# The chunk scan with compact states, 64x64 tiles and TensorE in the written order

## The chip, the core and the metric

The kernel runs on one core of one Trainium2 chip. The metric is the time of one execution on the device in microseconds (us). PE is TensorE, PEld its weight loads, DVE is VectorE, ACT ScalarE, POOL GpSimd, SP the engine that issues most transfers. Everything is float32. A product of two float32 operands stands in the trace as two matmul instructions, one after the other; a transpose is one.

## What is computed

The reference is a two-layer trunk over 512 latent and 256 context tokens of width 1024. The change touches one part of layer 0, the time mixing: eight heads of 64 features, each with a recurrence over the tokens, once forwards and once backwards.

```python
def rwkv7_scan(f, d, s0, reverse):
    def step(state, inp):
        r_t, w_t, k_t, v_t, kk_t, a_t = inp
        sa = jnp.einsum('bhvk,bhk->bhv', state, -kk_t)
        state = (state * w_t[:, :, None, :] + sa[..., None] * (kk_t * a_t)[:, :, None, :]
                 + v_t[..., None] * k_t[:, :, None, :])
        return state, jnp.einsum('bhvk,bhk->bhv', state, r_t)
    ...
    s_last, ys = lax.scan(step, s0, xs, reverse=reverse)
```

Before it stand the projections of the input and the factors r, w, k, v, kk, a; after it a group norm, a bonus, a gate, the output projection and the feed-forward block; then layer 1. The modulation of both layers (a product of the conditioning vector with 24 blocks of 512 columns) is computed beside.

## The kernel before

**Pairs and chunks.** The heads are worked on in four pairs (p = 0 to 3), two heads on the 128 partitions. The 768 tokens are cut into 12 chunks of 64, and the recurrence over a chunk is written as products of 64-row matrices. `chunks` (L983) walks the 12 chunks of a pair in both directions at once, in three steps per chunk:

1. `cha` gets the right-hand sides `pr` for both heads h and both directions d: four products of the chunk matrix Gs with Z (L1050) and two of AR with the state S (L1053); ACT copies them to `rr`. Then `pre_g` makes the chunk matrix Gs two chunks ahead: two products of 128 rows by 256 columns (L1003) against `bd`, a block-diagonal copy of AR that `pre_d` has ACT write (four copies for every two chunks), and a masked copy on DVE (L1005).
2. `chb` gets four 64x64 products of the inverse XI with `rr` (L1064); ACT copies them into Z in two halves, one per direction. Two products of AR with S start the output `py` (L1069). Every second chunk follow `pre_t` (four transposes, L1012) and `pre_v` (L1024).
3. `chb` gets two 128x128 products of bt with Z (L1076); four DVE instructions (L1086) make the next state S of them and of `sw`, which POOL scales before (L1081). Four products (L1092) finish the output, which ACT or DVE adds to y (L1100).

The state S is [128, 2, 128]: for each direction a 128x128 block in which only the two 64x64 blocks of the two heads are not zero. The chain from one chunk to the next is S, L1053, rr, L1064, Z, L1076, S.

**Tilings of the array.** The form in the trace names the rows and columns of the array that a product uses: 128*128 in L1003, L1012 and L1076, 128*64 in L1050, L1053, L1069, L1024 and L1092, 64*64 in L1064 and L903, 32*32 in L963 and L971, 128*2 in the modulation (L344), 2*128 in its transposition (L354).

**Beside the scan.** The loop over the pairs advances three generators: `cg`, the scan of pair p; `bg`, in 1.8 steps per step of `cg`, which holds `prep` of pair p+1 (chunk factors; L903 with a masked copy on DVE, L904, six times; an inverse by 62 small DVE instructions, L925 and L926, ended by a copy, L929; three trips of the blocks through DRAM; the merges L963 and L971), `mix_out` of pair p-1 and the first part of `prep` of pair p+2; and `ag`, the modulation (L344, 16 matmul instructions per step). The scan of pair p+1 needs the merged XI.

**What sets the order.** Outside blocks of a written order a scheduler puts each engine's instructions in order at build time, from priorities (the order in which the code runs), what is ready by its own estimate, and free buffers. At run time each engine works through its list and waits where an operand is missing. PSUM has eight banks here: two single tiles `one`, one pair of banks `wide` (L903 and others of `prep` use it), two single `cha`, one `chb` and one `pad` for the modulation.

## Time and profile before

| | us |
|---|---|
| median of 3 runs (2109.83 to 2113.08) | 2113.08 |
| span of the profiled execution | 2117.1 |
| scan of pair 0 to the start of pair 1 (383 to 482) | 99 |
| pair 1 (482 to 587.6) | 105.6 |
| pair 2 (587.6 to 677) | 89.4 |
| pair 3 (677 to 755) | 78 |
| the four pairs together | 372 |

The profiled execution's span is 4.0 us above the median, 0.2%; the two are not the same run. The edges of the four stretches are the first DVE instructions that write a state (L1088). A busy share of PE is read with care: a matmul that waits behind another for the array counts as busy, and its end is modelled.

### The profile page before, as it was taken

Reading aid. Unit: us, or ns where it says so; the run is one execution under the profiler, and the core shown is the slowest. Engines: PE = TensorE matmul, PEld = TensorE weight load, DVE = VectorE, ACT = ScalarE, POOL = GpSimd, SP = SyncE. Lnnn points to the kernel's source line nnn. Section 1 sums busy time; section 2 is a strip of 40 time slices with the busy share of each in tenths; the row PEclk is TensorE's granted clock in tenths of the full one; section 3 lists DMA queues with packets and bytes.
Section 4 is the critical chain, followed back from the end, with each engine's and each line's share of the span. In section 5 each row is a group of like instructions: output and inputs, shape, how many; then the busy total and the mean of one; then the engine's idle time right before and its main releaser. Section 6 shows DMA issues by size and latency. Waiting matters only on the chain.

```text
span 2117.1 us, 37174 instructions
## 1 busy us (share of the span) xinstructions
PE 2002.1 (95%) x15404; PEld 1674.9 (79%) x15404; DVE 1172.4 (55%) x2190; ACT 879.8 (42%) x1799; POOL 150.5 (7%) x202
## 2 busy tenths in 40 slices
PE   6899997989898999999999999989999899999997
PEld 4778875666665689888888889988878799888887
DVE  4575578565765438434334433674566656544445
ACT  3365533455454525332212222344677645322232
POOL 1000001112121100000000000001121000000000
PEclk7999998889898989999999999999999999999998
DMA  7432224544535624322212221134111424332231
GB/s 278 144 95 77 90 81 127 148 113 136 163 102 151 240 75 130 110 80 64 60 37 80 80 61 50 51 110 146 42 36 51 130 81 150 109 99 80 80 100 41
DMA packets 111434, 215.77 MB, mean 102 GB/s; under 512 B 38432, under 2 KB 63904, under 8 KB 110752
## 3 DMA queue, kind: packets, MB, share of 16 engines
q1 hardware_dynamic: 95968, 190.06, 28.9%
q10 hardware_dynamic: 15296, 23.33, 3.1%
q8 instruction: 121, 1.98, 0.4%
q14 instruction: 49, 0.40, 0.1%
HBM read 182.69 MB, written 28.05 MB: 100 GB/s over the span
## 4 chain that ended last, share of the span: by engine, by line
PE 80%; DVE 9%; ACT 4%; issue 3%; DMA 2%; POOL 1%; SPq 0%; ACTq 0%; POOLq 0%; DVEq 0%
PE x L1507 44%; PE x L422 9%; PE ax L522 3%; PE x L1003 2%; PE ax L503 2%; PE ad L344 2%; PE b L485 2%; PE chb L1076 1%; PE b L486 1%; PE cha L1092 1%; PE cha L1053 1%; PE chb L1064 1%; PE ad L354 1%; POOL r L258 1%; PE x L1012 1%
## 5 line engine op out<-in xcount | busy, mean ns | idle before, releaser
L179 ACT ACTIVATE w_hi<-w_raw 128x1024 fp32r<-128x1024 f32 x183 | 192.1, 1058 | 475.4 <-PE x L1507 362.7
L219 DVE TENSOR_TENSOR w_lo<-w_raw,w_hi 128x1024 fp32r<-128x1024 f32 x181 | 222.1, 1231 | 192.8 <-ACT w_hi L179 186.1
L1507 PE MATMUL x<-fl,w_hi 128*128 128x256 f32 (+1 forms) x864 | 291.7, 339 | 4.0 <-DVE fl L1594 3.9
L1507 PE MATMUL x<-uh,w_hi 128*128 128x512 f32 (+1 forms) x864 | 288.1, 339 | 3.0 <-ACT uh L179 3.0
L1507 PE MATMUL x<-fh,w_lo 128*128 128x256 f32 (+1 forms) x864 | 289.9, 337 | 0.0
L1507 PE MATMUL x<-ul,w_hi 128*128 128x512 f32 (+1 forms) x864 | 287.4, 336 | 0.0
L1507 PE MATMUL x<-uh,w_lo 128*128 128x512 f32 (+1 forms) x864 | 287.4, 335 | 0.0
L1507 PE MATMUL x<-fh,w_hi 128*128 128x256 f32 (+1 forms) x864 | 287.3, 338 | 0.0
L1521 DVE TENSOR_TENSOR oa<-x,oa 128x512 f32<-128x512 f32 (+1 forms) x184 | 103.0, 562 | 208.4 <-PE x L1507 207.8
L422 PE MATMUL x<-uh,w_hi 128*128 128x256 f32 (+1 forms) x560 | 188.4, 336 | 2.7 <-ACT po L179 2.3
L422 PE MATMUL x<-uh,w_lo 128*128 128x256 f32 (+1 forms) x560 | 187.6, 335 | 0.0
L422 PE MATMUL x<-ul,w_hi 128*128 128x256 f32 (+1 forms) x560 | 187.5, 335 | 0.0
L1507 PEld LDWEIGHTS x<-fl,w_hi 128*128 128x128 f32 x864 | 165.0, 191 | 22.4 <-DVE fl L1594 4.4
L1507 PEld LDWEIGHTS x<-fh,w_lo 128*128 128x128 f32 x864 | 164.7, 191 | 18.1
L1507 PEld LDWEIGHTS x<-uh,w_hi 128*128 128x128 f32 x864 | 161.9, 190 | 21.1 <-ACT uh L179 4.0
L1507 PEld LDWEIGHTS x<-fh,w_hi 128*128 128x128 f32 x864 | 162.5, 190 | 20.2 <-ACT fh L179 2.5
L1507 PEld LDWEIGHTS x<-uh,w_lo 128*128 128x128 f32 x864 | 163.0, 190 | 18.3
L1507 PEld LDWEIGHTS x<-ul,w_hi 128*128 128x128 f32 x864 | 162.7, 189 | 17.9
L422 PEld LDWEIGHTS x<-uh,w_hi 128*128 128x128 f32 x560 | 106.2, 190 | 11.8 <-ACT po L179 2.5
L422 PEld LDWEIGHTS x<-uh,w_lo 128*128 128x128 f32 x560 | 106.4, 190 | 9.2 <-issue 1.3
L422 PEld LDWEIGHTS x<-ul,w_hi 128*128 128x128 f32 x560 | 106.0, 189 | 8.8 <-issue 1.2
L1593 DVE TENSOR_TENSOR rl<-rl 128x512 f32<-128x512 f32 (+1 forms) x108 | 59.3, 550 | 75.5 <-ACT fh L179 75.3
(286 smaller groups left out, 3657.4 us busy)
## 6 DMA issues: line engine op xcount, KB each, us to landing
w_raw<-in_wf_dram SPq DMA_DIRECT2D x128, 512.0 KB
w_raw<-in_wada_dram SPq DMA_DIRECT2D x96, 512.0 KB
w_raw<-in_we_dram SPq DMA_DIRECT2D x21, 512.0 KB
w_raw<-in_wo_in_dram SPq DMA_DIRECT2D x18, 512.0 KB
w_raw<-in_wout_dram SPq DMA_DIRECT2D x16, 512.0 KB
hsc<-h ACTq DMA_DIRECT2D x8, 1024.0 KB
scr<-po ACTq DMA_DIRECT2D x21, 384.0 KB
h<-hsc SPq DMA_DIRECT2D x7, 1024.0 KB
```

The costliest lines, as they stand in the source:

```text
L179: return S.activation(o, i, f, **k)
L219: eng.tensor_tensor(o_lo, x, o_hi.bitcast(F32), op=ALU.subtract)
L258: G.tensor_tensor(dst, src, C["mhalf"][:, :n], op=ALU.pow)
L344: PE.matmul(ps[32 * j:32 * j + 2, 0:128], si[:, 2 * kp + k, :], w[:, k, j * 128:(j + 1) * 128], start=kp + k == 0, stop=kp == 3 and k == 1)
L422: PE.matmul(ps[:, 0:b - a], x, y, start=j == 0, stop=j == len(pairs) - 1)
L485: PE.matmul(ps[:, off:off + n], qs, kh, start=True, stop=False)
L503: PE.transpose(pt[:, (kb - k0) * 128:(kb - k0 + 1) * 128], P[:, kb * 128:(kb + 1) * 128], ident)
L522: PE.matmul(po[h * 64:h * 64 + 64, 0:128], v(h, k), pts[h][:, k], start=k == 0, stop=k == n - 1)
L1003: PE.matmul(pg[:, d].rearrange("p h t -> p (h t)"), BK[d][:, c, :], BD[:, i % 2, d].rearrange("p h t -> p (h t)"), start=True, stop=True)
L1507: PE.matmul(o, a, b, start=n == 0, stop=n == len(pairs) - 1)
L1521: tt(oa[:, m, tok], ps, oa[:, m, tok], op=ALU.add)
L1593: tt(r, r, r, op=ALU.mult)
```

## The change

Part by part (line numbers of after differ from those of before; the names don't):

- The state S becomes [128, 2, 64]: the heads on the two halves of the partitions, the block-diagonal zeros gone. `bd` and `pre_d` with its ACT copies go.
- `pre_g` makes Gs in eight products of 64 rows by 64 columns with 128 moving columns, over the four quadrants of the array, into the two banks of `wide` instead of one bank of `one`.
- The products of AR with S become four 64x64 products over the four quadrants for `pr` and four for `py`, both at the start of the chunk; `cha` takes two banks, one per head, and there is one `cha` instead of two.
- The products of Gs with Z for `pr` go ahead by a chunk (`pre_r`): ACT copies them to `r0`, and DVE adds the state's part (instead of an ACT copy of the sum).
- The two halves of Z are copied by ACT and by DVE (before: both by ACT).
- The products for the new state become four of 128 rows by 64 columns; two DVE instructions instead of four make S, and POOL's `sw` is issued in step 1 instead of step 3.
- `pre_v` stands in step 3, `pre_t` in step 2.
- In the loop over the pairs PE keeps the order in which the code is written; the other engines are ordered by the scheduler as before.

```diff
 def mix_state(sc):
-    SS = [sc.tile([128, 2, 128], F32, name=f"S{i}") for i in range(2)]
+    SS = [sc.tile([128, 2, 64], F32, name=f"S{i}") for i in range(2)]
...
-    def pre_d(ii):
-        for d, (c, e) in enumerate(pair(ii)):
-            for h in range(2):
-                hs = slice(h * 64, h * 64 + 64)
-                a = AR[d][hs, c:c + 2, :] if d == 0 else AR[d][hs, e:e + 2, :][:, ::-1, :]
-                act(BD[hs, :, d, h, :], a)
...
     def pre_g(i):
-        pg = one().rearrange("p (d h t) -> p d h t", d=2, h=2)
+        pg = wide().rearrange("p (h x) -> p h x", h=2)
         for d, c in enumerate((FWD[i], BWD[i])):
-            PE.matmul(pg[:, d].rearrange("p h t -> p (h t)"), BK[d][:, c, :], BD[:, i % 2, d].rearrange("p h t -> p (h t)"), start=True, stop=True)
+            for j in range(2):
+                for h in range(2):
+                    PE.matmul(pg[half(j), h, d * 128:d * 128 + 128], BK[d][half(h), c, half(j)], AR[d][half(h), c, :], start=True, stop=True)
...
+    def pre_r(i):
+        pz = one()[:, 0:128]
+        for h, d in HD:
+            PE.matmul(pz[half(d), half(h)], nxt["G", i][:, d, h, 0:64], ZZ[i // 2 % 2][:, i % 2, d, h, :], start=True, stop=True)
+        r0 = ct.tile([128, 128], F32, name="r0", bufs=2)
+        act(r0, pz)
...
-        cha = pch.tile([128, 512], F32, name="cha", bufs=2)
+        cha = pch.tile([128, 2, 512], F32, name="cha")
...
+        if i:
+            for h, d in HD:
+                PE.matmul(cha[half(d), h, 0:64], AR[d][half(h), cd[d], 0:64], St[half(h), d, :], start=True, stop=True)
+            r0, rr = rr, ct.tile([128, 128], F32, name="rr")
+            tt(rr.rearrange("p (h v) -> p h v", h=2), cha[:, :, 0:64], r0.rearrange("p (h v) -> p h v", h=2), op=ALU.add)
+            for h, d in HD:
+                PE.matmul(cha[half(d), h, 64:128], AR[d][half(h), cd[d], 64:128], St[half(h), d, :], start=True, stop=False)
...
-        act(Zt[64:128, 1].rearrange("p h v -> p (h v)"), pu[64:128, 0:128])
+        V.tensor_copy(Zt[64:128, 1].rearrange("p h v -> p (h v)"), pu[64:128])
...
             for d in range(2):
-                PE.matmul(pd[:, d * 128:d * 128 + 128], bt[:, s, d, :], Zt[:, d].rearrange("p h v -> p (h v)"), start=True, stop=True)
+                for h in range(2):
+                    PE.matmul(pd[half(h), half(d)], bt[:, s, d, half(h)], Zt[:, d, h, :], start=True, stop=True)
...
+                    stt(Sn[:, d, :], pd[:, half(d)], w, sw[:, d, :], op0=ALU.mult, op1=ALU.add)
...
+            if i + 1 < NCH:
+                pre_r(i + 1)
...
-            for _ in cg:
+            with tc.manual_schedule(engines={mybir.EngineType.PE}):
+                for _ in cg:
...
```

On PE, in a chunk of pair 0 in the middle of the scan, before (S and ar are the state and AR, bd the block-diagonal copy, the numbers behind names are buffers, ad is the modulation):

```order
L1012 MATMUL x_4325<-con,bk_2925 128x128
L1092 MATMUL cha<-Z_3500,Gs 64x64
L1012 MATMUL x_4325<-con,bk_2925 128x128
L1076 MATMUL chb<-Z_3500,bt 128x128 x2
L1092 MATMUL cha<-Z_3500,Gs 64x64 x3
L1012 MATMUL x_4325<-con,bk_2926 128x128 x2
L344 MATMUL ad<-w_raw,si 2x128 x8
L1050 MATMUL cha<-Z_3501,Gs 64x64 x4
L1003 MATMUL x_4387<-bd,bk_2925 128x256
L1053 MATMUL cha<-S_3499,ar_2923 64x128
L1003 MATMUL x_4387<-bd,bk_2926 128x256
```

and the same chunk's work after, where L1001 is `pre_g`, L1011 `pre_t`, L1070, L1080 and L1090 the products for Z, for S and for the output, and L1032 `pre_r`:

```order
L1001 MATMUL b_4288<-ar_2923,bk_2925 64x128 x4
L1001 MATMUL b_4288<-ar_2924,bk_2926 64x128 x4
L1070 MATMUL chb<-rr,XI 64x64 x4
L1011 MATMUL x_4311<-con,bk_2925 128x128 x2
L1011 MATMUL x_4311<-con,bk_2926 128x128 x2
L1080 MATMUL chb<-Z_3500,bt 64x64 x4
L1090 MATMUL cha<-Z_3500,Gs 64x64 x4
L1032 MATMUL x_4352<-Z_3501,Gs 64x64 x4
```

The tiling changed at nearly every row; now one run of 64*64 (L1056 and L1060 stand ahead of it), the transposes, and one run of 128*64 follow each other, and the next chunk's products with Z stand in the same run.

On PE, at the end of pair 0 and the start of pair 1, before (b is the `wide` tile, xw and XI are operands of the merges):

```order
L1050 MATMUL cha<-Z_3500,Gs 64x64 x4
L903 MATMUL b_4951<-ar_4898,bk_4900 64x64 x5
L963 MATMUL x_4720<-xw,XI 32x32
L963 MATMUL x_4747<-xw,XI 32x32
L903 MATMUL b_4951<-ar_4898,bk_4900 64x64 x3
L1050 MATMUL cha<-Z_3500,Gs 64x64 x4
L903 MATMUL b_4961<-ar_4898,bk_4900 64x64 x8
L903 MATMUL b_4997<-ar_4898,bk_4900 64x64 x8
L903 MATMUL b_5068<-ar_4899,bk_4901 64x64 x8
L963 MATMUL x_4720<-xw,XI 32x32 x23
L963 MATMUL x_4747<-xw,XI 32x32 x23
L903 MATMUL b_5093<-ar_4899,bk_4901 64x64 x8
```

and after:

```order
L1032 MATMUL x_4841<-Z_3500,Gs 64x64 x3
L963 MATMUL x_4848<-xw,XI 32x32 x24
L963 MATMUL x_4875<-xw,XI 32x32 x24
L344 MATMUL ad<-w_raw,si 2x128 x8
L1070 MATMUL chb<-rr,XI 64x64 x4
L971 MATMUL x_4918<-XI,xw 32x32 x24
L971 MATMUL x_4945<-XI,xw 32x32 x24
L354 MATMUL ad<-con,adar 128x2 x4
L344 MATMUL ad<-w_raw,si 2x128 x8
L1090 MATMUL cha<-Z_3501,Gs 64x64 x4
```

The products L903 of the pair after next stood between the first and the last merges; now they follow the first chunk of the new pair, and the last chunk's L1070 and L1090 stand between and behind the merges.

On DVE, in the fifth chunk of pair 0, after (pr and X are the steps of the inverse, S the state, rr the right-hand sides):

```order
L926 TENSOR_TENSOR X<-X,pr 96x4x28
L925 TENSOR_TENSOR pr<-X,N 96x135
L926 TENSOR_TENSOR X<-X,pr 96x5x27
L1084 SCALAR_TENSOR_TENSOR S_3498<-chb,wc,sw 128x64
L925 TENSOR_TENSOR pr<-X,N 96x156
L1084 SCALAR_TENSOR_TENSOR S_3498<-chb,wc,sw 128x64
L926 TENSOR_TENSOR X<-X,pr 96x6x26
L925 TENSOR_TENSOR pr<-X,N 96x175
L926 TENSOR_TENSOR X<-X,pr 96x7x25
L1058 TENSOR_TENSOR rr<-cha,r_4257 128x128
```

The steps of the inverse, one after the other, lie between the instructions of the scan's chain, as they did before; the chain has the two state instructions and rr there where it had four state instructions.

## Rows read from the trace of the kernel before

**Rows 1.** The page: busy time of PE, and the chain that ended last, by engine.

```profile
PE 2002.1 (95%) x15404; PEld 1674.9 (79%) x15404; DVE 1172.4 (55%) x2190; ACT 879.8 (42%) x1799; POOL 150.5 (7%) x202
...
PE 80%; DVE 9%; ACT 4%; issue 3%; DMA 2%; POOL 1%; SPq 0%; ACTq 0%; POOLq 0%; DVEq 0%
```

**Rows 2.** Busy us by pair: PE, PEld, DVE, ACT, POOL; granted clock, DMA share, GB/s.

```profile
383.00:482.00 99.00, 93.08 (x1170) 63.73 (x1168) 63.49 (x162) 51.14 (x133) 18.88 (x24) 0.90 0.38 109
482.00:587.60 105.60, 97.27 (x1282) 69.59 (x1281) 70.81 (x175) 52.69 (x137) 21.82 (x24) 0.89 0.51 149
587.60:677.00 89.40, 77.28 (x972) 54.23 (x970) 53.71 (x150) 39.25 (x112) 18.84 (x21) 0.90 0.40 118
677.00:755.00 78.00, 76.42 (x917) 51.58 (x914) 37.73 (x88) 42.84 (x112) 13.01 (x20) 0.91 0.59 200
349.00:755.00 406.00, 370.31 (x4764) 259.22 (x4765) 244.73 (x610) 198.72 (x522) 73.65 (x91) 0.88 0.50 150
```

**Rows 3.** Timeline of PE in pair 2: start, duration, line, tiles, form, instructions.

```profile
600.53 0.45 PE L1064 MATMUL chb<-rr,XI 64*64 64x64 f32 x8
600.91 0.44 PE L1069 MATMUL cha<-S,ar 128*64 128x128 f32 x4
601.18 0.27 PE L1024 MATMUL x<-con,vr 128*64 128x128 f32 x1
...
602.69 0.70 PE L1003 MATMUL x<-bd,bk 128*128 128x256 f32 x2
603.32 0.62 PE L344 MATMUL ad<-w_raw,si 128*2 128x128 f32 x16
603.87 0.71 PE L1076 MATMUL chb<-Z,bt 128*128 128x128 f32 x4
604.51 0.45 PE L1092 MATMUL cha<-Z,Gs 128*64 128x64 f32 x8
604.89 0.62 PE L344 MATMUL ad<-w_raw,si 128*2 128x128 f32 x16
605.45 0.45 PE L1050 MATMUL cha<-Z,Gs 128*64 128x64 f32 x8
605.73 0.69 PE L1053 MATMUL cha<-S,ar 128*64 128x128 f32 x4
606.34 0.48 PE L1003 MATMUL x<-bd,bk 128*128 128x256 f32 x1
```

**Rows 4.** Timeline of PE around the end of pair 0; brackets: idle time and its releaser.

```profile
458.01 0.70 PE L1092 MATMUL cha<-Z,Gs 128*64 128x64 f32 x8
...
468.50 1.12 PE L903 MATMUL b<-ar,bk 64*64 64x64 f32 x16 [2.93 <-DVE XI L904]
469.55 2.76 PE L963 MATMUL x<-xw,XI 32*32 32x32 f32 x92
...
478.96 0.69 PE L1064 MATMUL chb<-rr,XI 64*64 64x64 f32 x8
```

**Rows 5.** Groups on DVE in 349 to 760: busy us, mean ns, idle before.

```profile
L1086 DVE SCALAR_TENSOR_TENSOR S<-chb,wc,sw 64x64 f32<-64x64 f32 x160 | 45.3, 283 | 56.0 <-PE chb L1076 51.4 <-ACT bd L179 1.1
...
L925 DVE TENSOR_TENSOR pr<-X,N 96x60 f32<-96x60 f32 (+15 forms) x100 | 32.7, 327 | 1.3
...
L904 DVE TENSOR_TENSOR XI<-b,con 64x512 f32<-64x512 f32 x18 | 12.4, 687 | 7.8 <-PE b L903 7.7
```

**Rows 6.** Groups on ACT in 349 to 760, same columns.

```profile
L179 ACT ACTIVATE Z<-chb 64x128 f32<-64x128 f32 x96 | 25.9, 270 | 25.6 <-PE chb L1064 24.2
...
L179 ACT ACTIVATE rr<-cha 128x128 f32<-128x128 f32 x48 | 13.3, 276 | 49.0 <-PE cha L1053 44.1 <-PE cha L1050 4.4
```

**Rows 7.** The chain ahead of pair 0's scan: start us, us, what.

```profile
363.41 0.99 DVE N L929
...
373.20 2.76 PE x L963 x92
```

**Rows 8.** Two stretches of 10 us, columns as in rows 2.

```profile
660.00:670.00 10.00, 6.60 (x208) 5.87 (x208) 0.00 (x0) 2.89 (x6) 0.00 (x0) 0.50 0.91 274
...
690.00:700.00 10.00, 10.00 (x142) 6.93 (x142) 5.87 (x13) 7.26 (x19) 1.20 (x2) 1.00 0.91 302
```

More of the change, by code (lines that the diff above doesn't have):

```diff
@@ L1027, in pre_v @@
                 act(Zt[o:o + 64, :, d].rearrange("p s h v -> p s (h v)"), pv[o:o + 64])
-        pre_d(0)
+        def pre_r(i):
[4 more added lines that the diff above has]
+            act(r0, pz)
+            nxt["r", i] = r0
         pre_g(0)
@@ L1036, in chunks @@
         pre_v(0)
+        pre_r(0)
         yield "begin"
         St = None
[L1039 removed]
         for i in range(NCH):
             ii, s = divmod(i, 2)
[L1042 removed]
+            Gs, bt, rr = nxt["G", i], nxt["t", ii], nxt["r", i]
             cd = (FWD[i], BWD[i])
             Zt = ZZ[ii % 2][:, s]
[L1045 removed]
+            cha = pch.tile([128, 2, 512], F32, name="cha")
             chb = pch.tile([128, 512], F32, name="chb")
[L1047 to L1050 removed]
+            pu, pd = chb[:, 0:128], chb[:, 128:256]
             if i:
[L1052 to L1055 removed]
+                for h, d in HD:
[4 more added lines that the diff above has]
+                    PE.matmul(cha[half(d), h, 64:128], AR[d][half(h), cd[d], 64:128], St[half(h), d, :], start=True, stop=False)
+                sw = ct.tile([128, 2, 64], F32, name="sw", bufs=2)
+                if i < NCH - 1:
+                    for d in range(2):
+                        G.tensor_scalar(sw[:, d], St[:, d, :], wc[:, d, cd[d]:cd[d] + 1], None, op0=ALU.mult)
             if i + 2 < NCH:
                 pre_g(i + 2)
[L1058 to L1059 removed]
             yield
@@ L1062, in chunks @@
                 for d in range(2):
-                    ds = slice(d * 64, d * 64 + 64)
-                    PE.matmul(pu[ds, h * 64:h * 64 + 64], XI[ds, cd[d], h, :], rr[ds, h * 64:h * 64 + 64], start=True, stop=True)
-            act(Zt[0:64, 0].rearrange("p h v -> p (h v)"), pu[0:64, 0:128])
-            act(Zt[64:128, 1].rearrange("p h v -> p (h v)"), pu[64:128, 0:128])
-            if i:
-                for d in range(2):
-                    PE.matmul(py[d * 64:d * 64 + 64, 0:128], AR[d][:, cd[d], 64:128], St[:, d, :], start=True, stop=False)
-            if ii < 5:
-                (pre_t, pre_v)[s](ii + 1)
+                    PE.matmul(pu[half(d), half(h)], XI[half(d), cd[d], h, :], rr[half(d), half(h)], start=True, stop=True)
+            act(Zt[0:64, 0].rearrange("p h v -> p (h v)"), pu[0:64])
+            V.tensor_copy(Zt[64:128, 1].rearrange("p h v -> p (h v)"), pu[64:128])
+            if s and ii < 5:
+                pre_t(ii + 1)
             yield
@@ L1079, in chunks @@
                     if i:
[L1080 to L1088 removed]
+                        stt(Sn[:, d, :], pd[:, half(d)], w, sw[:, d, :], op0=ALU.mult, op1=ALU.add)
+                    else:
+                        ts(Sn[:, d, :], pd[:, half(d)], w, None, op0=ALU.mult)
                 St = Sn
@@ L1091, in chunks @@
                 for d in range(2):
-                    PE.matmul(py[d * 64:d * 64 + 64, h * 64:h * 64 + 64], Gs[:, d, h, 64:128], Zt[:, d, h, :], start=not i, stop=not i or h == 1)
+                    PE.matmul(cha[half(d), h, 64:128], Gs[:, d, h, 64:128], Zt[:, d, h, :], start=not i, stop=True)
+            if s == 0 and ii < 5:
+                pre_v(ii + 1)
+            if i + 1 < NCH:
+                pre_r(i + 1)
             for d in range(2):
@@ L1453, in trunk @@
             t = None
-            for _ in cg:
-                n += 1
-                due[0] += RATE3
-                while due[0] >= 1:
-                    due[0] -= 1
-                    t = next(bg, None)
-                if t != QUIET:
-                    due[1] += RATE4
-                while due[1] >= 1:
-                    due[1] -= 1
-                    next(ag, None)
-            n = 3 * NCH
-            for t in bg:
-                if t != QUIET:
-                    next(ag, None)
+            with tc.manual_schedule(engines={mybir.EngineType.PE}):
+                for _ in cg:
+                    n += 1
+                    due[0] += RATE3
+                    while due[0] >= 1:
+                        due[0] -= 1
+                        t = next(bg, None)
+                    if t != QUIET:
+                        due[1] += RATE4
+                    while due[1] >= 1:
+                        due[1] -= 1
+                        next(ag, None)
+                n = 3 * NCH
+                for t in bg:
+                    if t != QUIET:
+                        next(ag, None)
             if p < 3:
```

41 lines of the change are left out of this document (11 added, 30 removed).

## The prediction

> **What bounds the kernel now.** I read the page first: PE is busy 95% of the span and 80% of the chain that ended last lies on it [rows 1]. A busy share does not say what the engine is busy with, so I went on to the windows by pair. In the scan of the four pairs PE is busy 93, 97, 77 and 76 us of 99, 106, 89 and 78: 344 of 372. DVE has 63, 71, 54 and 38 [rows 2]. PE is the bound, and the other engines wait for it: DVE stood idle 56 us ahead of the state's instructions, nearly all for L1076; ACT 49 us ahead of `rr`, for L1053 and L1050 [rows 5, 6].
>
> Then the timeline of PE, for what fills those 344 us. Eight instructions of L1050 reach the next run in 0.28 us where that run (L1053) has the same tiling, and the eight of L1092 in 0.38 where it has another (starts 605.45 to 605.73 and 604.51 to 604.89) [rows 3]. So the end of a tiling costs 0.10. The first weight load of a run can't be hidden behind the run ahead; with about 0.06 for it, a change of tiling costs 0.16. (0.28 − 0.06)/4 = 0.055 is then a round: two tiles side by side, 64 moving columns, one of the two instructions of a product each. With 128 columns a round is 0.11; L1069's four instructions, two such rounds, and the change behind them took 0.27, which bears this out [rows 3]. PE changes its tiling some ten times a chunk: much of its time goes to changes and to 128-wide products that are half zeros.
>
> Last, the end of pair 0: from its last L1092 (458.01) to pair 1's first L1064 (478.96) are 21 us without progress of either scan. L903 stands ahead of the merges and waited 2.93 us for DVE's L904 [rows 4]. The chain ahead of pair 0 shows what the trip through DRAM costs by itself: the inverse's last copy (L929) ends at 364.4, the merges begin at 373.2, 8.8 us [rows 7].
>
> **The change, part by part.** First PE's work in one chunk; start to start, from [rows 3]. Before: Gs twice 0.63 (1.26), L1053 0.61, L1069 0.27, L1076 0.64, L1050 0.33 (half of its runs end with a change, my choice), L1092 0.38, L1064 0.38: 3.87. After: one run of 64x64 with four products for `pr` and four for `py` (each two rounds, 0.11) and eight for Gs (four rounds of 128 columns, 0.44) and one change, 0.82; the products for Z, 0.38 as L1064; one run of 128x64 with the products for S, for the output and with Z of the next chunk (0.22 each) and one change, 0.82. Together 2.02. Transposes and `pre_v` are the same in both. Saved 1.85 a chunk, 22 a pair.
>
> The least sure term in it: that four quadrants work at once. No row shows this; [rows 3] show two 64x64 tiles (L1064). If only two work at once, the first run has twice the rounds, 0.82 becomes 1.48, and 1.19 a chunk is saved, 14 a pair. I take the first, because the two tiles of L1050 and of L1064 do overlap in these rows. The Trainium skill ("TensorEngine Tiling (Array Packing)", Key Properties) says that a change of the mode drains the array and that different tiles load and multiply in parallel. The 0.10 above agrees with the first half; on the second for four quadrants no row here decides; by that sentence the run would cost 0.82, without it 1.48.
>
> DVE, per chunk: two state instructions less (−0.57), the addition `rr` more (0.28, by ACT's `rr`) and half of Z (0.27, by ACT's) [rows 5, 6]. Neither stands on DVE in the trace: from below by half a state instruction, 0.14 each, from above by L925's 0.33. The net is −0.3 to +0.1, taken as 0: DVE stays at 63, 71, 54, 38. ACT loses the copies to `bd`, `rr` and half of Z and gains `r0`; with at most 53 us in a pair [rows 2] it binds nowhere, and the loss is hidden. POOL's `sw` moves from step 3 to step 1, off the chain. It was not what DVE waited for [rows 5], so it is worth 0; if POOL were late, S would be. No transfer is added, and SP's queue keeps its content. Pair 3 moves 78 x 200 = 15.6 MB [rows 2]; at the 302 GB/s seen [rows 8] that is 52 us, below which it can't get if those transfers stay in it.
>
> So PE alone would need 71, 75, 55 and 54 us, 256 in all; DVE is below that in every pair, but close in the first three. What is then late next? The chain S, `pr`, `rr`, Z, S, which now has DVE in three places. In the written order PE waits at `pr`'s, Z's and S's products, and behind them wait Gs, the transposes and the modulation, on which others wait in turn. On DVE a step of the inverse or of `prep` may stand ahead of each of the three; I price each with one L925, 0.33 [rows 5]: 1.0 a chunk, 12 a pair. Two of the six hand-offs L903 to L904 of the single `wide`, which Gs now shares, at 0.69 [rows 5]: 1.4. Between 0 (all hidden) and six (4). That makes 13 for each of pairs 0 to 2: 84, 88, 68. Pair 3 has no inverse beside it; I give it 8: 62.
>
> The boundary is inside this: in the new order L903 no longer stands ahead of the merges, and the inverse ends on DVE some three chunks before the last, so 3 x 7 us lie over the 8.8 of transfers. If that cover failed, 9 us at each of three boundaries would come back, 27.
>
> Sum: 84 + 88 + 68 + 62 = 302 against 372, a gain of 70. Off it goes the clock. At 660 to 670 us PE was busy 6.6 of 10 us and the granted clock was 0.50, the lower of its two levels, 1.2 GHz; at 690 to 700 it was busy throughout at 1.00 [rows 8]. PE's busy share of the scan falls from 344/372, 92%, to 256/302, 85%. I take 20 us more at the lower level, 10 us of time, with 0 and 35 as ends. The gain is 60: span 2117 − 60 = 2057; the span of the profile lies 4 above the median, so the median is 2113 − 60 = 2053.
>
> **The rivals.**
> - Only two quadrants at once: 8 us less in pairs 0 to 2, where DVE is the next bound and covers part (−6), and 8 in pair 3: 2053 + 17 to 30, say 2073. For it: no row with four. Against it: the two tiles of L1050, and of L1064, work at once.
> - Everything hidden: the chain lies under PE's and DVE's work, the clock holds. 71 + 75 + 55 + 58 = 259, gain 113, 2000. Against it: idle ahead of S and `rr` in [rows 5, 6] shows that the engines do wait for each other.
> - The lower clock for much more of the scan: a mean of 0.70 instead of 0.88 [rows 2] makes 256 into 321; with 35 of waits 356, gain 16, 2097. For it is [rows 8]; against it, that waits of about 0.3 to 0.7 us leave no long holes.
> - Slower: PE's written order meets DVE's other work. A chunk took 372/48 = 7.75 us; PE needs 256/48 = 5.3. Waits of over 2.4 us a chunk turn the gain into a loss. If each of the three DVE instructions on the chain stands behind one L904 and one L925 (0.69 + 0.33), that is 3.05 a chunk with nothing to fill it: 8.4 x 48 = 401, 29 more, 2142. For it: the scheduler did fill such holes with other products before; the written order can't, and DVE's list has the inverse between the chain's instructions. Against it: six L904 a pair are not enough for three in each chunk, and the long `prep` operations end before the inverse.
> - Issue-bound: after has 12 products more per chunk, about 1,118 matmul instructions in all, 4,764 + 1,118 = 5,880 in the stretch [rows 2]. L344's sixteen took 0.55, 0.034 each [rows 3]: 200 us, no bound. Were the price that of L1069's four, 0.27/4 = 0.068, they would take 400, and with 35 of waits less the 406 of the stretch now, the time would be 29 more: 2142. A chance of 1 in 100, since L344's row speaks against it. The Trainium skill ("TensorE: Matmul & The Clock Gate", "Wait — 56ns, not 53.3ns?") names some 62 ns per MATMUL with hardware decode off; by that estimate 5,880 would take 365 us. The 0.034 of L344 contradicts it here.
> - The change does nothing, because PE's work wasn't the bound: 2113. Against it stand 344 of 372.
>
> **How the numbers follow.** Forecast 2053, 0.56 (its own range 2025 to 2085: 1.0 a chunk of waits may be 0.5 or 1.5, and the clock's 10 may be 0 or 30). Two quadrants 0.13, all hidden 0.08, low clock 0.08, slower 0.12, issue 0.01, nothing 0.02. About 0.2% is what a measurement of this kernel can tell from no change. Faster takes the first three, most of the low clock and a margin off: 0.81; same 0.05; slower 0.14. The range leaves out the slower cases (0.13) and the fast half of "all hidden" (0.04): 2003 to 2100.
>
> **What would show it.** Right: the sixteen instructions of L1001 in some 0.5 us, four of them starting together; about 5.3 us of PE a chunk and chunks of 7 us; the merges directly behind the last chunk, with no hole of 21 us; DVE at about 75% in pairs 0 and 1; pair 3 above 52; a granted clock of 0.85 or so. Two quadrants: L1001 at 0.9 and over. Slower or little gain: PE's idle time ahead of L1070, L1080 and L1056, released by DVE, of over 2 us a chunk, or a mean clock of 0.7. The prediction is wrong at its root if PE's busy time in the scan does not fall by some 80 us.

## The result: slower by 3.2%, and the profile after

The changed kernel took 2181.57 us, median of four runs (2173.40 to 2189.43), against 2113.08 for the kernel before: a ratio of 1.032 with an interval of 1.029 to 1.036. 2053 was forecast. The profiled execution has a span of 2183.0, against 2117.1.

From the page of the changed kernel: busy time, the granted clock in 40 slices, the chain that ended last. For the kernel before, [rows 1] has the first and the third.

```profile
PE 1997.2 (91%) x16508; PEld 1684.3 (77%) x16508; DVE 1170.0 (54%) x2194; ACT 826.9 (38%) x1655; POOL 132.2 (6%) x199
...
PEclk9999996656667769999999999999999999999998
...
PE 54%; DVE 3%; ACT 2%; issue 2%; POOL 1%; DMA 0%; POOLq 0%; ACTq 0%; DVEq 0%; SPq 0%
```

PE is as busy as before (2002), though there is less to do; the slices 7 to 15 (327 to 819 us), the scan and the stretch ahead of it, stand out by their clock. The stretches of the four pairs and of the scan as a whole, as in [rows 2]: time, then busy us of PE, PEld, DVE, ACT, POOL, granted clock, DMA share, GB/s.

```profile
375.40:504.36 128.96, 104.79 (x1554) 78.10 (x1550) 64.87 (x165) 40.12 (x106) 15.70 (x24) 0.60 0.35 106
504.36:633.14 128.78, 102.48 (x1480) 71.90 (x1482) 70.17 (x175) 37.90 (x94) 16.98 (x24) 0.64 0.35 106
633.14:737.27 104.13, 82.35 (x1388) 62.67 (x1383) 57.63 (x156) 27.89 (x82) 12.64 (x21) 0.71 0.38 115
737.27:822.42 85.15, 67.09 (x1142) 49.23 (x1140) 37.23 (x92) 31.88 (x82) 10.76 (x20) 0.76 0.64 214
...
375.40:822.42 447.02, 356.72 (x5554) 261.90 (x5550) 229.90 (x586) 137.79 (x362) 56.09 (x89) 0.67 0.41 129
```

The scan took 447 us instead of 372, +75; the stretch ahead of it 8 less (26 for 34), the rest 2 less: +66, the whole difference. In the scan PE was busy 357 us (344 before) and idle 90 (28 before), and the mean clock fell from 0.90 to 0.67.

Busy time times clock is a rough measure of the work that PE had: 344 x 0.90 = 310 before, 357 x 0.67 = 239 after. The forecast took 88 us of 344 off, which by the same measure is 79; measured are 71. The measure is rough because the clock is the mean of the whole stretch, idle time included; with the clock of the busy time alone the trace gives 313 and 229, 84 less. So the work did go, and two things ate more than it: **idle time and the lower clock**. Where they arise, two stretches of pair 0 in the timeline show (PE, and one row of DVE). In the first the granted clock was 1.0, in the second 0.5:

```profile
417.33 0.34 PE L1056 MATMUL cha<-S,ar 64*64 64x64 f32 x8
418.53 0.34 PE L1060 MATMUL cha<-S,ar 64*64 64x64 f32 x8 [0.86 <-DVE rr L1058]
418.70 0.62 PE L1001 MATMUL b<-ar,bk 64*64 64x128 f32 x16
419.14 0.41 PE L1070 MATMUL chb<-rr,XI 64*64 64x64 f32 x8
419.48 0.66 PE L1011 MATMUL x<-con,bk 128*128 128x128 f32 x4
421.21 0.45 PE L1080 MATMUL chb<-Z,bt 128*64 128x64 f32 x8 [1.08 <-DVE Z L1072]
...
459.76 0.69 PE L1070 MATMUL chb<-rr,XI 64*64 64x64 f32 x8
460.38 2.92 PE L859 MATMUL b<-al,la 64*128 64x512 f32 x4
...
460.80 0.29 DVE L1072 COPY Z<-chb 64x128 f32<-64x128 f32 x1
...
463.23 1.03 PE L344 MATMUL ad<-w_raw,si 128*2 128x128 f32 x16
464.20 0.69 PE L1080 MATMUL chb<-Z,bt 128*64 128x64 f32 x8
```

The sixteen instructions of L1001 pass in 0.44 us (418.70 to 419.14), what the sum had for four quadrants at once. But L1060 comes after 0.86 us of idle time that DVE's `rr` ended, and L1080 after 1.08 that DVE's half of Z ended. Some 40 us later, at the lower clock, 3.8 us of other products (L859 of the preparation, L344 of the modulation) stand between L1070 and L1080 because the code stands so; DVE had copied Z at 461.1, and L1080 came at 464.2. PE's idle time of the whole scan, ahead of three groups of the chain (busy us, mean ns, idle before and its releasers):

```profile
L1080 PE MATMUL chb<-Z,bt 128*64 128x64 f32 x352 | 26.5, 292 | 14.4 <-DVE Z L1072 14.2
L1056 PE MATMUL cha<-S,ar 64*64 64x64 f32 x352 | 19.7, 282 | 8.5 <-DVE y L1103 3.8 <-DVE S L1084 2.3 <-ACT y L179 2.0
L1060 PE MATMUL cha<-S,ar 64*64 64x64 f32 x352 | 18.6, 292 | 28.9 <-DVE rr L1058 28.8
```

L1060 computes with S and AR, not with `rr`. But it writes other columns of the same `cha` that DVE reads for `rr`, and its idle time ends when that read does. The Trainium skill ("PSUM — Partial Sum Buffer", PSUM bank collisions raise a hardware error) says that two engines must not be on the same bank and partitions at the same time, so the program has to keep them apart. The trace agrees as far as it goes: of the 28.9 us ahead of L1060, 28.8 end with DVE's `rr`; no run put the two into separate banks.

That they share a bank is not new. `pr` and `py` lay side by side in one bank of `cha` before, too; but there L1069, the product for `py`, stood behind the products for Z, and `rr` had long been read. It never waited:

```profile
L1069 PE MATMUL cha<-S,ar 128*64 128x128 f32 x176 | 22.2, 310 | 0.0
```

What is new is its place, right behind `pr`. L1056 pays for the single `cha` in a like way: 5.8 of its 8.5 us end when DVE or ACT has read the output of the chunk before out of it, for y.

The other 38 us of PE's idle time stand for the most part, 36 us, ahead of products beside the scan. The three largest groups, and L903 of the kernel before behind them:

```profile
L903 PE MATMUL b<-ar,bk 64*64 64x64 f32 x288 | 16.1, 270 | 10.8 <-DVE XI L904 5.9 <-DVE Gs L1003 4.9
L407 PE MATMUL b<-con,t 128*128 128x128 f32 x12 | 3.0, 425 | 6.8 <-DVE t L404 6.8
L344 PE MATMUL ad<-w_raw,si 128*2 128x128 f32 x1232 | 66.7, 361 | 5.9 <-DVE mod L356 5.9
```

```profile
L903 PE MATMUL b<-ar,bk 64*64 64x64 f32 x192 | 11.5, 272 | 10.7 <-DVE XI L904 10.7
```

In the kernel before, 20 of its 28 us of idle time in the scan stood ahead of such products.

### The profile page after: what moved, and what is told of

It is laid out like the page before. It is cut to its first block, busy times and chain, and to the rows that moved or that the text cites. A ratio compares the mean times of both kernels' runs of the same rounds, so it can differ in the third digit from the quotient of the medians.

```text
span 2183.0 us, 39210 instructions
## 1 busy us (share of the span) xinstructions
PE 1997.2 (91%) x16508; PEld 1684.3 (77%) x16508; DVE 1170.0 (54%) x2194; ACT 826.9 (38%) x1655; POOL 132.2 (6%) x199
## 4 chain that ended last, share of the span: by engine, by line
PE 54%; DVE 3%; ACT 2%; issue 2%; POOL 1%; DMA 0%; POOLq 0%; ACTq 0%; DVEq 0%; SPq 0%
PE x L1512 43%; PE x L422 5%; PE ax L522 2%; PE ax L503 1%; PE b L485 1%; PE b L486 1%; DVE nacc L282 1%; ACT P L179 0%; POOL r L258 0%; POOL rs L258 0%; DVE h L304 0%; PE ax L265 0%; PE ax L523 0%; PE ax L274 0%; ACT w_hi L179 0%
```

## The experiments

Theory A: the written order on PE costs the time. PE waits where the code stands while work that it could do meanwhile stands elsewhere. Theory B: PE has so little work left that the chain through DVE sets the time in any order. Later a third came in, C: the preparation of the next pair bounds. Ratios are to the kernel before, measured beside each run, with intervals. The kernel before itself took 2110 to 2120 in these sessions, so a difference in us between kernels of different sessions is good to some 5 to 10 us. Idle time, busy time and clock are those of the scan's four pairs in each profile. L numbers shift a little from kernel to kernel; the tiles name the products.

### The order on PE

**Scheduler instead of written order** (e1_sched), on the changed kernel:

```diff
-            with tc.manual_schedule(engines={mybir.EngineType.PE}):
+            with ExitStack():
                 for _ in cg:
...
```

> The changed kernel, but in the loop over the pairs the scheduler orders PE's instructions, as it did before the change; the compact states and the tilings stay. Theory A (the written order is the cause: it leaves PE idle behind rr, Z and S in every chunk, and the granted clock sits at the lower level for it): PE's idle time in the scan falls from 88 us to 40 or less, the mean granted clock rises from 0.66 to 0.80 or more, time 2050 to 2120. Theory B (the work that was taken off PE is the cause: PE has too little left to do whatever the order): clock below 0.72, time 2160 to 2190.

2096.05, 0.990 (0.988 to 0.993).

```profile
379.27:735.07 355.80, 312.77 (x5324) 221.95 (x5320) 217.45 (x577) 134.71 (x351) 59.39 (x89) 0.86 0.47 151
```

As theory A said: idle 43 instead of 90, clock 0.86. With its order taken away the change gains, but 1%, not 3%. Part of the rest can be counted in the timelines of PE: the tiling changes 454 times in this scan, 266 times in the changed kernel (497 before), since the scheduler pulls the runs apart. 188 changes more at the forecast's 0.16 are 30 us; busy times clock is 313 x 0.86 = 269 against 239, also 30. The two scans don't hold quite the same products (5,320 and 5,554 instructions), so this is no more than a rough agreement.

**Written order on the kernel before** (e2_before_order), the opposite edit:

```diff
-            for _ in cg:
+            with tc.manual_schedule(engines={mybir.EngineType.PE}):
+                for _ in cg:
...
```

> The kernel before, with one edit: PE keeps the written order in the loop over the pairs; block-diagonal states and tilings as before. Theory A: its chain a chunk then stands open on PE as in the changed kernel, idle time rises by 40 us or more, clock below 0.80, time 2150 to 2250. Theory B: PE has its old work, clock 0.85 or more, time 2105 to 2135.

2153.98, 1.016 (1.012 to 1.021).

```profile
379.71:776.00 396.29, 332.77 (x4487) 237.45 (x4483) 235.25 (x583) 187.39 (x496) 71.92 (x89) 0.90 0.46 141
```

The order alone costs the old kernel 1.6%. Idle time rises by 35 to 63, a little less than A said, but the clock stays at 0.90, which A did not say.

**Only the scan's own products keep the written order** (e11_hybrid_after). Each is issued behind the one before it in the scan's list; the products beside the scan are placed among them by the scheduler:

```diff
-            with tc.manual_schedule(engines={mybir.EngineType.PE}):
+            with ExitStack():
...
+        last = [None]
+        def behind():
+            return tc.issue_after(last[0].ins) if last[0] else ExitStack()
...
-                PE.matmul(pz[half(d), half(h)], ...
+                with behind(): last[0] = PE.matmul(pz[half(d), half(h)], ...
```

> The changed kernel with the order of the scan's own products unchanged, word for word, but only that: the products beside the scan (preparation of the next pair, modulation, output of the pair before) are placed among them by the scheduler instead of at the places where the code stands. If the beside products' fixed places cost the time (they stand between two links of the chain while PE waits elsewhere): PE's idle time falls from 90 to 50 us, clock to 0.80, time 2090 to 2120. If the order of the scan's own products costs it (L1060 ahead of the products for Gs): 2150 to 2185.

2101.27, 0.993 (0.989 to 0.996).

```profile
381.55:735.94 354.39, 298.31 (x5368) 223.83 (x5364) 223.43 (x580) 136.35 (x355) 56.78 (x89) 0.81 0.47 150
```

80 us less than the changed kernel, with the scan's products in exactly its order: idle 56 instead of 90, clock 0.81, and the same work (298 x 0.81 = 241, 239 there). The idle time ahead of the chain's three groups fell from 52 to 28, that ahead of the products beside the scan from 36 to 27. So these 80 us are the price not of the scan's own order but of **the fixed places of what stands beside it**: of the 93 us that the scan lost (the stretch ahead of it grew by 6), 34 are idle time and 58 busy time, by the clock.

**The modulation fixed too** (e18_ag_fixed): as e11, and the modulation's products keep their written places.

```diff
+                with after_last(): last[0] = PE.matmul(ps[32 * j:32 * j + 2, 0:128], si[:, 2 * kp + k, :], ...
```

> e11_hybrid_after, but the modulation's products (L344, L354 of the changed kernel) are held at their written places among the scan's products too; only the preparation and the output of the pair before stay with the scheduler. The changed kernel, with all three fixed, took 2182, e11_hybrid_after, with all three free, 2101. If the modulation's fixed places cost the 80 us: 2150 to 2185. If the preparation's do (its products wait for DVE while the scan's stand behind them, and they take up to 2.9 us between two links of the chain): 2095 to 2125.

2141.39, 1.016 (1.012 to 1.020). Neither number. The modulation's places account for about half (40 of 80 us by the medians, 48 of 83 by the ratios); that the rest is due to the places of the preparation and of the output follows by subtraction; no run fixed them alone.

```profile
375.60:773.48 397.88, 313.82 (x5523) 230.30 (x5519) 227.40 (x584) 136.98 (x362) 55.98 (x89) 0.78 0.45 144
```

Of its groups on PE, the products of S for the output:

```profile
L1065 PE MATMUL cha<-S,ar 64*64 64x64 f32 x352 | 17.0, 268 | 34.4 <-DVE rr L1063 34.4
```

The wait for `rr` is 34.4 us (10.2 in e11, 28.9 in the changed kernel): L344 could have filled it and stands elsewhere.

**The same on the kernel before** (e13_before_hybrid): the lines of e11 in the old `chunks`, beside products with the scheduler as ever.

> The kernel before (block-diagonal states, old tilings) with the scan's own products held in their written order and the products beside it still placed by the scheduler, as e11_hybrid_after does with the changed kernel. If the scan's own order is harmless and e2_before_order lost its 1.6% to the fixed places of the beside products: 2100 to 2125. If the scan's order costs by itself: 2135 to 2160.

2110.69, 0.998 (0.996 to 1.000): the scan's own order is harmless, and what e2 lost it lost to the fixed places as well.

### The clock

**Products that nobody reads** (e3_fill), in the waits of the changed kernel:

```diff
+                PE.matmul(chb[:, 256:512], ident, C['mg'][:, 0:256], start=True, stop=True)
                 for h, d in HD:
                     PE.matmul(cha[half(d), h, 64:128], AR[d][half(h), cd[d], 64:128], ...
...
+            if i:
+                pf = one()
+                PE.matmul(pf[:, 0:256], ident, C['mg'][:, 0:256], start=True, stop=True)
+                PE.matmul(pf[:, 256:512], ident, C['mg'][:, 0:256], start=True, stop=True)
             if i < NCH - 1:
```

> The changed kernel with three products of 128 rows by 256 columns added per chunk that nobody reads: one behind the state's products for pr (ahead of L1060, which waits for rr) and two ahead of the products for the new state (L1080, which wait for Z). It measures the price of the clock. Each takes some 0.4 us at the upper level, 44 x 3 x 0.4 = 53 us of PE's time in all. If the lower clock is what costs the time (A and B alike): clock 0.80 or more in the scan, and the time falls in spite of the added work, to 2100 to 2150. If the chain's waits cost it and the clock is only a sign of them: 2180 to 2240.

2165.28, 1.023 (1.020 to 1.026): 16 us faster than the changed kernel, with 132 products more. The clock is as expected for a price of its own, 0.89, the time 15 us above the range given for it.

```profile
380.15:802.67 422.52, 357.02 (x5819) 252.88 (x5815) 229.96 (x586) 137.25 (x362) 55.49 (x89) 0.89 0.42 136
```

PE is busy for as long as in the changed kernel to a third of a microsecond (357.0, 356.7) and has done 357 x 0.89 = 318 of work instead of 239; the products that nobody reads stand where it was idle, and idle time is 66 instead of 90. The clock is no mere sign of the waits: at 0.67 the same busy time carries a quarter less.

### The order of the scan's own products

**L1060 behind the products for Gs** (e4_py_late), otherwise the changed kernel with its written order:

```diff
-                for h, d in HD:
-                    PE.matmul(cha[half(d), h, 64:128], AR[d][half(h), cd[d], 64:128], St[half(h), d, :], start=True, stop=False)
...
             if i + 2 < NCH:
                 pre_g(i + 2)
+            if i:
+                for h, d in HD:
+                    PE.matmul(cha[half(d), h, 64:128], AR[d][half(h), cd[d], 64:128], St[half(h), d, :], start=True, stop=False)
```

> The changed kernel with one move in the written order: the four products of AR with S for the output (L1060 in the changed kernel), which wait 27.7 us in all for DVE's rr, stand behind the eight products for Gs instead of ahead of them. Theory A: the products for Gs fill the wait for rr, most of the 27.7 us goes, time 2145 to 2165, clock some 0.05 higher. If that wait only moves to the next instruction of the chain (L1070 needs the same rr): 2175 to 2185.

2140.09, 1.011 (1.008 to 1.014), 41 us less from one moved run, more than either range had.

```profile
373.24:767.25 394.01, 312.11 (x5555) 226.82 (x5551) 227.47 (x586) 137.08 (x362) 58.34 (x89) 0.79 0.45 145
```

The moved group on PE:

```profile
L1067 PE MATMUL cha<-S,ar 64*64 64x64 f32 x352 | 16.2, 259 | 10.1 <-DVE rr L1058 9.4
```

Its wait fell by 19 us, from 28.9 to 10.1, but more than half of that came up elsewhere, 8 us at the other links (Z 18.0 instead of 14.4, S and y 13.3 instead of 8.5): idle time is 82, only 8 less. The other 45 us of the 53 that the scan lost are busy time, by the clock (0.79).

**pre_v and pre_r into the wait for Z** (e5_fill_z), on e4; **and both halves of Z on ACT** (e6_z_act), on e5:

```diff
-            V.tensor_copy(Zt[64:128, 1].rearrange("p h v -> p (h v)"), pu[64:128])
+            act(Zt[64:128, 1].rearrange("p h v -> p (h v)"), pu[64:128])
             if s and ii < 5:
                 pre_t(ii + 1)
+            if s == 0 and ii < 5:
+                pre_v(ii + 1)
+            if i + 1 < NCH:
+                pre_r(i + 1)
...
```

> e4_py_late with one more move in the written order: pre_v and pre_r (products for the next chunks, of the same tiling as the products for S) stand right behind the products for Z, ahead of the products for S, which wait 18.0 us for DVE's half of Z in e4_py_late. If waits of the written order and the clock that falls with them set the time: 10 us or more of that idle time goes, the mean clock of the scan rises above 0.79, time 2110 to 2130 (e4_py_late 2140). If the chain through DVE sets it, whatever PE does meanwhile: PE's products for S start as late as before, 2135 to 2145.

> e5_fill_z with both halves of Z copied by ACT, as before the change, instead of one by DVE. If DVE's queue is what makes the second half late (the steps of the inverse stand ahead of it): 10 us or more less than e5_fill_z. If the order of PE alone matters: within 5 us of it; ACT's second copy starts 0.27 us after the first, so no more than 48 x 0.3 = 14 us slower.

2145.60, 1.015 (1.011 to 1.019), and 2136.48, 1.011 (1.008 to 1.013). Neither account of e5 holds as it stood: the products for S wait 13 us less, and the time is no shorter. The wait only moves: 18.0 ahead of the products for S became 5.4, 13.3 ahead of L1056 became 24.5, of which 16 are for y.

```profile
L1085 PE MATMUL chb<-Z,bt 128*64 128x64 f32 x352 | 22.4, 256 | 5.4 <-DVE Z L1073 5.2
L1056 PE MATMUL cha<-S,ar 64*64 64x64 f32 x352 | 19.3, 266 | 24.5 <-DVE y L1104 11.9 <-DVE S L1089 7.5 <-ACT y L179 4.4
```

Within one written list, work taken from one gap leaves another open. DVE's copy of Z costs 9 us at most, just short of the 10 expected; the intervals of e5 and e6 overlap.

**The same orders with the beside products free**: e9_hybrid is e4 with e11's edit, e10_hybrid_zact is that with Z on ACT, e12_hybrid_e6 is e6 with e11's edit, e17_hybrid_e5 is e5 with it; e8_z_act_s is e1 with Z on ACT.

> The same freeing of the beside products, on e4_py_late's order of the scan's products (L1060 behind those for Gs). The scan keeps its runs of one tiling, so fewer changes than e1_sched's 454. If those changes are what e1_sched lost of the forecast gain: 350 changes or fewer and 2060 to 2085, below e1_sched's 2096. If the preparation or the chain through DVE bounds the pairs: 2090 to 2105 as e1_sched.

> e9_hybrid with both halves of Z copied by ACT. Chain through DVE is the bound: 5 to 12 us less than e9_hybrid. PE or the preparation: within 4 us.

> e10_hybrid_zact with pre_v and pre_r ahead of the products for S (as e6_z_act, whose beside products are freed here). In the written order this move took 13 us off the wait for Z and put 9 on the wait for S and y, no gain. If a chain of fixed length bounds: within 5 us of e10_hybrid_zact. If PE's waits: 5 to 15 us less.

> e12_hybrid_e6 with the second half of Z copied by DVE again, as in the changed kernel. If DVE's queue ahead of that copy lengthens the chain: 2085 to 2095 against 2077. If the preparation bounds the pairs, as the boundaries of e15_half_inv say: within 6 us of 2077.

> e1_sched with both halves of Z copied by ACT. If DVE's queue lengthens the chain from chunk to chunk: 5 to 15 us less than e1_sched. If the preparation or PE bounds the pairs: within 4 us of e1_sched.

| | us | ratio (interval) | changes of tiling | idle, busy, clock |
|---|---|---|---|---|
| e11_hybrid_after | 2101.27 | 0.993 (0.989 to 0.996) | 323 | 56, 298, 0.81 |
| e9_hybrid | 2087.74 | 0.987 (0.984 to 0.990) | 286 | 65, 276, 0.86 |
| e10_hybrid_zact | 2099.35 | 0.992 (0.989 to 0.995) | 283 | 59, 292, 0.81 |
| e12_hybrid_e6 | 2076.94 | **0.981 (0.978 to 0.985)** | 305 | 48, 278, 0.86 |
| e17_hybrid_e5 | 2078.86 | 0.986 (0.982 to 0.989) | 307 | 54, 289, 0.84 |
| e8_z_act_s | 2093.97 | 0.992 (0.989 to 0.995) | 407 | 45, 305, 0.85 |

e12 beats both kernels, 36 us below the kernel before and 105 below the changed one, from the same arithmetic. Who copies Z decides nothing (e12 and e17, e8 and e1 lie within 3 us, as expected of the preparation or PE as the bound; e10 is 12 slower than e9, where 4 at most were expected, for no reason that I found, and the intervals overlap). pre_v and pre_r ahead of S, no gain with the fixed places, is worth 22 us without them in one pair of kernels (e12 against e10, more than either range) and 9, within the intervals, in the other (e17 against e9). L1060 behind the products for Gs is worth 14 (e9 against e11) instead of 41. e9 has the few changes of tiling that were expected, 286, but its time lies between the two ranges. Its scan holds nearly the products of e1's, with 168 changes less and 276 x 0.86 = 237 of work against 269: 32 us, 27 at 0.16 a change.

### What bounds the pairs then

In e9 PE is idle 65 us, and yet pairs 0 to 2 took 97, 100 and 85 us, hardly less than before (99, 106, 89). The end of pair 0 in e12_hybrid_e6, on PE and DVE, shows why; e1 and e9 read alike.

```profile
442.57 0.27 DVE L1094 SCALAR_TENSOR_TENSOR S<-chb,wc,sw 128x64 f32<-128x64 f32 x1
...
447.00 1.06 DVE L929 COPY N<-X 96x1024 f32<-96x1024 f32 x1
...
447.28 0.22 PE L1076 MATMUL chb<-rr,XI 64*64 64x64 f32 x1
...
458.40 2.77 PE L963 MATMUL x<-xw,XI 32*32 32x32 f32 x96
...
468.77 0.48 DVE L1096 TENSOR_SCALAR S<-chb,wc 128x64 f32<-128x64 f32 x2 [9.08 <-ACT r L179]
```

The scan's last product for Z ends at 447.5, the inverse's copy at 448.1; then come 10 us of transfers until the merges at 458.4 and 10 more until the next pair's first state. In the changed kernel the copy had ended at 453.2, 24 us ahead of the last state (476.9), and the merges came at 486.8. A faster scan has caught up with the preparation: theory C. In pair 0 it is new; in pairs 1 and 2 the inverse's copy had ended 1 and 3 us behind the last state in the kernel before, too.

**Half of the inverse left out** (e15_half_inv on e12, e16_after_half_inv on the changed kernel): 32 of its 62 DVE instructions.

```diff
+            if s < 15:
-            pr = iv.tile([128, 256], F32, name="pr")
+                pr = iv.tile([128, 256], F32, name="pr")
...
```

> e12_hybrid_e6 with the last 16 of the 31 steps of the inverse left out (32 of 62 small DVE instructions; the steps of the program around them keep their places, the numbers that come out are not the reference's). If the preparation's chain bounds pairs 0 to 2: 8 to 12 us less in each and as much ahead of pair 0, 2030 to 2045. If PE or the chain from chunk to chunk bounds them: only the part ahead of pair 0, 2062 to 2072.

> The changed kernel with the same 16 steps of the inverse left out (numbers that come out are not the reference's). There the inverse's copy ended 24 us ahead of the scan's last state in pair 0 and the merges stood behind the scan on PE. Written order as the bound: 8 to 14 us less (ahead of pair 0, and a shorter queue on DVE), 2165 to 2175. Preparation as the bound there too: 2135 to 2150.

e15: 2056.25, 0.972 (0.967 to 0.976), 21 us less than e12, between the two expectations. Its pairs, and those of e12 behind them:

```profile
369.26:458.79 89.53, 84.03 (x1502) 60.90 (x1499) 50.27 (x122) 42.35 (x113) 15.01 (x24) 0.82 0.50 158
458.79:544.75 85.96, 76.40 (x1532) 56.09 (x1528) 55.83 (x131) 43.01 (x115) 17.94 (x24) 0.98 0.53 167
544.75:614.98 70.23, 62.70 (x1346) 47.87 (x1346) 42.30 (x115) 28.18 (x87) 13.41 (x21) 0.95 0.60 179
614.98:691.82 76.84, 64.25 (x1147) 47.24 (x1143) 35.16 (x79) 36.19 (x96) 8.55 (x20) 0.85 0.60 212
```

```profile
380.51:468.77 88.26, 77.25 (x1502) 58.49 (x1498) 58.27 (x154) 41.66 (x112) 17.31 (x24) 0.86 0.47 146
468.77:560.64 91.87, 79.75 (x1446) 59.58 (x1442) 64.49 (x159) 41.45 (x107) 19.43 (x24) 0.83 0.43 134
560.64:644.77 84.13, 69.57 (x1466) 52.25 (x1463) 50.54 (x146) 30.65 (x95) 13.69 (x21) 0.88 0.58 187
644.77:706.78 62.01, 51.65 (x972) 38.90 (x967) 34.02 (x75) 33.73 (x88) 11.98 (x20) 0.87 0.58 196
```

Pairs 0 to 2 took 246 us instead of 264. The stretch from a pair's last state to the next pair's first fell from 25.9, 25.7 and 28.6 us to 18.0, 16.1 and 16.2, 30 us in all, so there the preparation does bound; the chunks ahead of it took 11 us longer. 11 more are won ahead of pair 0, as the pair's start shows (369.3, 380.5). But pair 3 is 15 us longer: PE ran 1,147 instructions in it instead of 972. The counts say that work which PE has to do in any case had stood in the waits for the preparation. C holds for the ends of the pairs, and only in part for the total.

e16: 2145.09, 1.012 (1.009 to 1.016), 36 less than the changed kernel, where 8 to 14 or 31 to 46 were expected. The number fits the second, the preparation as the bound; the pairs don't. The profiled execution, the slowest of the four, is 27 us shorter than that of the changed kernel: 16 us lie ahead of pair 0 (its first state at 359.7 instead of 375.4) and 15 in pair 0, whose clock is 0.78 instead of 0.60; pairs 1 and 2, which C would shorten, took 128 and 105 where the changed kernel took 129 and 104.

```profile
359.74:473.20 113.46, 86.10 (x1554) 64.20 (x1550) 55.65 (x134) 42.59 (x109) 16.05 (x24) 0.78 0.41 128
473.20:601.27 128.07, 103.68 (x1478) 73.72 (x1480) 60.65 (x143) 38.13 (x94) 17.22 (x24) 0.62 0.35 110
601.27:706.46 105.19, 83.55 (x1387) 62.49 (x1383) 47.86 (x125) 27.70 (x80) 12.84 (x21) 0.69 0.37 114
```

**The preparation earlier** (e7_rate on e1, 2.4; e14_rate on e12, 2.2):

```diff
-RATE1, RATE2, RATE3, RATE4 = 2.0, 1.5, 1.8, 1.2
+RATE1, RATE2, RATE3, RATE4 = 2.0, 1.5, 2.4, 1.2
```

> e1_sched (the scheduler orders PE) with one number changed: the work beside the scan advances 2.4 steps per step of the scan instead of 1.8. In e1_sched pairs 0 to 2 took 98, 101 and 88 us, no less than before the change, though the scan itself was some 20 us shorter: the chain of the preparation (transfers, the inverse on DVE, transfers, merges) ends last there. If that is the bound: the inverse starts earlier and time falls to 2070 to 2088. If PE's changes of tiling bound these pairs (454 of them, 497 before, 266 in the written order): 2090 to 2105.

> e12_hybrid_e6 with the work beside the scan advanced 2.2 steps per step of the scan instead of 1.8. In e12_hybrid_e6 the last product of a pair's scan for Z ends at 447.5 and the merges begin at 458.4; the inverse's copy ends at 448.1: the pair waits for the preparation. If that bounds pairs 0 to 2: 5 us less in each, 2055 to 2070. If PE has the same work to do in any case: 2070 to 2085.

2105.68, 0.997 (0.995 to 0.999), and 2074.16, 0.980 (0.977 to 0.984). e7 is slower than e1, by 0.6% of the kernel before; it won 6 and 11 us in pairs 0 and 2 and lost 18 in pair 1, at a clock of 0.73; e14 is 3 us from e12, as expected if PE has the same work in any case. To start the preparation earlier does not help. I take it that it takes DVE and PE from the scan that it runs beside; no run shows that apart from the clock.

## Why the prediction was wrong

**What fills PE, and the price of a tiling: right.** L1001 in 0.44 settles the term that was called least sure, four quadrants: its sixteen instructions start in fours, at 418.70, 418.81, 418.92 and 419.03. The rival with two at a time is out. The Trainium skill's sentence on tiles that work in parallel ("TensorEngine Tiling (Array Packing)", Key Properties) agrees with the row. The issue-bound rival is out too: those sixteen instructions took 0.028 each. The some 62 ns that the Trainium skill ("TensorE: Matmul & The Clock Gate", "Wait — 56ns, not 53.3ns?") names for hardware decode off are not in this row. A change at 0.16 fits, roughly, what e1 lost against the changed kernel (30 us for 188) and against e9 (32 for 168). One reading behind it was off: the 0.27 of L1069 were said to hold a change, but L1024 behind it has the same tiling; they are two rounds and a first weight load. PE's work in the scan fell by 71 us, or 84 by the busy time's clock, where 79 were forecast.

**DVE's load at no change: right.** 65, 70, 58 and 37 us by pair against 63, 71, 54 and 38; a state instruction 279 ns, `rr` 290, the copy of Z 294, where 0.28, 0.28 and 0.27 had been taken.

**Waits of 1.0 us a chunk on the chain: the size right, one place wrong.** L1060, L1080 and L1056 waited 28.9 + 14.4 + 8.5 = 51.8 us, 1.1 a chunk. That the sum agrees is partly luck: each of the three had been given the same 16. And the prediction had L1056, L1060 and L1001 as one run without a wait inside. It missed that `py` now stands right behind `pr`, in the bank that DVE still has to read, and that the run's longest part, Gs, stands behind that wait instead of filling it. e4 prices this: 41 us.

**The rest of the idle time: the step that failed.** Besides the chain the sum had 4 us, the hand-offs of `wide`; measured are 90 − 52 = 38, 36 of them ahead of products beside the scan. 20 us of such waits stood in the kernel before already, and the sum, which began from PE's busy time alone, did not carry them over. It asked who keeps the chain's products waiting, and looked on DVE, where the slower rival had its price too. It did not ask what stands beside the scan's products on PE itself. The excerpts of the order showed L344, L963 and L971 between the chain's products, and the prediction read there only that L903 no longer stood ahead of the merges. With PE in the written order such products neither fill a wait nor step aside: 80 us by e11, idle time and clock together, about half of them the modulation's (e18).

**The clock: mis-sized by a factor of nine, and the larger part of the error.** 10 us were taken, 35 at most. 239 of work take 357 us at 0.67 and would take 266 at the 0.90 of before: 91. The forecast was 302 + 10 = 312 for the scan, 46 of it idle. Measured were 447: 44 more of idle time and 91 more busy, which is the whole error of 135. The low-clock rival had the right clock (0.70), but with 35 us of waits, and so came out at 2097; it and the slower rival had been priced apart, and happened together. The sign by which the prediction was to be wrong at its root, a busy time of PE that does not fall by some 80 us, misleads for the same reason: busy time rose from 344 to 357 while the work fell.

**The hole at the boundary: wrong.** 21 us were to close because the inverse ends early. It did in pairs 0 and 1, 24 and 27 us ahead of the last state (5 in pair 2), but in the written order the merges waited on PE behind the scan's last products and the next pair's first: in pair 0 last state 476.9, first of the next pair 504.4, 27.5 us; before it was some 28. Where the merges are free (e12), the inverse is no longer early.

The slower rival's general sentence, that the scheduler filled holes which the written order can't, is what e1, e2 and e11 show. It got 0.12 because its price was looked for on the wrong engine.

**Open** is what sets the clock. PE was busy 80% of the scan in the changed kernel, 79% in e4 and 81% in e9, and was granted 0.67, 0.79 and 0.86; 84% in e2 and e3 went with 0.90 and 0.89. The busy share alone does not tell.

## What to carry to other kernels

A written order on one engine is an order for everything that engine does. Hold the products whose runs matter in order among themselves and leave the work beside them to the scheduler; here that alone turned 3.2% slower into 0.7% faster, and with three moves in the scan's own order and Z on ACT it became 1.9%. When a change takes work off a busy engine, price the idle time and the clock together: less work in the same gaps can run slower, and an unread product in a gap is a cheap way to find out. And when a product moves up behind another that writes the same bank, look who reads the bank in between.

## What the runs showed of the hardware

Adding 132 unread products to the scan made it 25 us shorter (447 to 423): the products stood in what had been idle time (90 us before, 66 with them), and PE's busy time stayed the same, because the mean granted clock went from 0.67 to 0.89. I had taken a lower clock for a loss of some per cent that follows from waits, not for one that a little more work takes away.
